# Moving the start addresses of pools by 32 or 64 bytes in a two-layer decoder kernel

## The chip, the cores and the metric

The kernel runs on one core of one Trainium2 chip. The metric is the device time of one execution in microseconds (us). The kernel before takes 2033.95 us, the median of three runs (2031.35 to 2036.37).

## What is computed

Two decoder layers on a sequence of 512 tokens with 1024 features, all in float32. Each layer is a half-step SwiGLU feed-forward network (FFN), a token mixer, and a second half-step FFN. The mixer of layer 0 is a short gated convolution, that of layer 1 a sparse attention with 16 heads in 4 groups.

```python
for i in range(DEPTH):                                # 2 layers
    h = adaln(x, norm_g[i, 0], shift[:, 0], scl[:, 0])
    x = x + HALF * gate[:, 0, None, :] * swiglu(h, ffn_w_in[i, 0], ffn_w_out[i, 0])
    h = adaln(x, norm_g[i, 1], shift[:, 1], scl[:, 1])
    y = short_conv_mixer(...) if i % 2 == 0 else nsa_mixer(...)
    x = x + gate[:, 1, None, :] * y
    h = adaln(x, norm_g[i, 2], shift[:, 2], scl[:, 2])
    x = x + HALF * gate[:, 2, None, :] * swiglu(h, ffn_w_in[i, 1], ffn_w_out[i, 1])
```

`swiglu` is `(silu(h @ w_g) * (h @ w_u)) @ w_out` with an inner width of 2816, which is 22 blocks of 128.

## The kernel before

**Data.** Everything is held transposed: a tile has 128 features on the partitions and 512 tokens along the free dimension, so that one partition of such a tile is 2048 bytes. Each float32 operand is split into a high and a low part (`split`, L163 to L165: ScalarE copies the high part, VectorE subtracts for the low part), and one product of two such operands is three matmuls, high by high, low by high and high by low (`mm3`, L167 to L170). In a name such as `gu<-hhi,whi` the profile gives the output, then the streamed operand (`hhi`), then the operand that is held in the array (`whi`). The streamed operand has 256 or 512 columns of 4 bytes, the held one has 128 columns, 512 bytes on a partition. `project` (L184) runs the three matmuls over the 8 blocks of 128 features.

**Stages in order.** FFN 0 (`ffn_first`), convolution (`conv`), FFN 1 and FFN 2 (`ffn`), attention (`nsa` with `compressor`, `attend`), FFN 3 (`ffn`). TensorE runs one instruction list in the order in which the scheduler put it.

**FFN 1, 2 and 3.** The first three of the 22 blocks are multiplied plainly (`head_start` and `pair`, matmuls of 256 columns, with `hs` and `gu` as outputs). The other 19 go through `seven_products` (L471): the two halves of the inner dimension and of the tokens make a 2 by 2 by 2 product that is done with seven products instead of eight, each of 4 by 3 = 12 matmuls of 256 columns. That makes 84 matmuls for each block j, 57 such blocks in the kernel, in this order: two products of `hhi`/`hlo` with `whi`/`wlo`, four of `th`/`tl` with `qah`/`qal` or `qbh`/`qbl`, and one of `hhi`/`hlo` with `qbh`/`qbl`. The blocks come in four parts (3, 6, 6 and 4 blocks). After each of the first three parts stand 144 matmuls of 512 columns, `y<-ahi/alo,whi/wlo`, which multiply the part's result by the output weights; after the last part the same work is done in matmuls of 256 columns (`ty`).

**FFN 0 and the convolution** use plain matmuls of 512 columns (`gu`, `y`, `cv`), with weights that come in turn from the common pool `wp` and from a pool of their own (`ap`).

**Pools.** Tiles lie in pools that are stacked from the left end of the memory (`cst`, `wp`, `tp`, `sp`, then `ada` or `hp`, `hw`, `sw`, `nw`, ...) and from its right end (`fa`, `tt`, `swa`, `tf`, `cva`, `na`, `ow`). A tile begins at the next multiple of 32 bytes, so the start of a tile within 128 bytes follows from the sizes of all that lie outside it. Those places are written here as two numbers, streamed/held: 96/64 says that the streamed tile begins 96 bytes and the held one 64 bytes behind a multiple of 128. Further columns or blocks of these tiles lie multiples of 512 bytes further on, so one pair of numbers holds for all matmuls of a product.

Of the kernel before, what the change touches and what calls it, by code (L numbers as in the profile page):

```python
# [12 lines left out]
F32 = mybir.dt.float32  # L13
F32R = mybir.dt.float32r
I32 = mybir.dt.int32
AF = mybir.ActivationFunctionType
# [5 lines left out]
P = 128  # L22
# [10 lines left out]
HD = 64  # L33
# [19 lines left out]
def decoder_kernel(ctx, tc, xT, cT, ng, adaw, adab, ffi, ffo, cwi, cw, cwo,  # L53
                   nwi, nwg, pos, w1, w2, qg, kg, nwo, rb, onehot, rowok, out):
    nc = tc.nc

    def pool(es, name, bufs, **kw):
        kw.setdefault("reuse_waits", "tile")
        return es.enter_context(tc.tile_pool(name=name, bufs=bufs, **kw))

    cst = pool(ctx, "cst", 1)
    wp = pool(ctx, "wp", 4)
    tp = pool(ctx, "tp", 1)
# [14 lines left out]
    def tmp(name, n=T, tag="t"):  # L78
        bufs, size = TAGS[tag]
        return tp.tile([P, n], F32, name=name, tag=tag, padded_shape=[P, size], bufs=bufs)  # L80
# [3 lines left out]
    ap = ada_es.enter_context(tc.tile_pool(name="ada", bufs=4))  # L84
# [6 lines left out]
    nc.sync.dma_start(cond, bass.AP(tensor=cT.tensor, offset=cT.offset, ap=[[0, P], [1, D]]))  # L91
    nc.gpsimd.dma_start(ngs, ng)
    nc.gpsimd.dma_start(adabs, adab)
    one = ap.tile([P, 1], F32, name="one", bufs=1)
    nc.vector.memset(one, 1.0)
    nc.scalar.activation(one, one, AF.Silu)
    ident = cst.tile([P, P], F32, name="ident")
    make_identity(nc, ident)
    ones = cst.tile([P, P], F32, name="ones")
# [1 line left out]
    cws = cst.tile([P, 3 * KD], F32, name="cws")  # L101
    qgs = cst.tile([P, 1], F32, name="qgs")
    kgs = cst.tile([P, 3], F32, name="kgs")
    rowm = cst.tile([P, 1], F32, name="rowm")
    mods = cst.tile([P, NSUB * NMOD], F32, name="mods")

    nc.scalar.activation(cond, cond, AF.Silu)
# [55 lines left out]
    def split(src, hi, lo):  # L163
        nc.scalar.activation(hi, src, AF.Copy)  # L164
        nc.vector.tensor_tensor(lo, src, hi, ALU.subtract)  # L165
# [6 lines left out]
    def weights(src, nk, ncol, own=None, held=3, raws=None, to=None):  # L172
        def part(name, dt, bufs, from_):
            return (from_ or wp).tile([P, nk * ncol], dt, name=name, tag=name, padded_shape=[P, KD * P], bufs=bufs)

        hi, lo = to or (part("whi", F32R, held, own), part("wlo", F32R, held, own))
        raws = raws or own
        raw = part("wraw", F32, 3 if raws in (None, wp) else 2, raws)
        nc.sync.dma_start(raw.rearrange("p (a n) -> p a n", a=src.shape[1]), src)
        split(raw, hi, lo)  # L180
        return [t.rearrange("p (k n) -> p k n", n=ncol) for t in (hi, lo)]
# [160 lines left out]
    def head_start(nrm, h, jobs):  # L342
        os = [psum("hs") for _ in jobs]
        for hf, (a, b) in enumerate(HALVES):
            with tc.high_priority():
                for d in range(KD):
                    nrm.piece(d, hf)
            for k in range(KD):
                for o, job in zip(os, jobs):
                    w, wc, kw = job(k)  # L350
                    project(o[:, a:b], w, wc, h, [(kw, k)], k == 0, k == KD - 1, a, b)
        return os
# [109 lines left out]
    def ffn(s, f, nrm, nxt, w0, ahead):  # L462
        with ExitStack() as es:
# [69 lines left out]
            with ExitStack() as tf_es:  # L533
                nrm.alloc_seven(hp, pool(tf_es, "tf", 1), tt)
                h = nrm.hi, nrm.lo
                with ExitStack() as hw_es:
                    hw = pool(hw_es, "hw", 1)
                    w = w0 + [weights(ffi[f, j, c], KD, P, hw, 1, wp) for j, c in js[len(w0):]]
                    os = head_start(nrm, h, [(lambda k, w=w_: (w, 0, k)) for w_ in w])
                os += pair(f, nj, h, halves=True)  # L540
                nrm.quarters()
            nj += 1
            sw_es = es.enter_context(ExitStack())
            sw = pool(sw_es, "sw", 1)
            for j in range(nj):
                hid.activate(os[2 * j], os[2 * j + 1])
            for p, (j0, j1) in enumerate(FOUR):
                for j in range(max(j0, nj), j1):
                    seven_products(j)
                n = j1 - j0  # L550
# [116 lines left out]
    def nsa_in(c, own=None, held=2):  # L667
        return [weights(nwi[c, kh], KD // 2, CW, own if kh else None, held if kh and own else 3, wp if held == 1 else None)
                for kh in range(2)]

    def nsa(s, nrm, nxt, w0, ahead):
        with ExitStack() as es:
# [46 lines left out]
            def squares():  # L719
                return sp.tile([P, 16], F32, name="vq")  # L720
# [57 lines left out]
            Q = [na.tile([P, T], F32R, name=f"q{q}") for q in range(NG)]  # L778
            keys, heads = turners(qn, kn, K, Q)
            with ExitStack() as hw_es:  # L780
                wv = nsa_in(5, pool(hw_es, "hw", 1), 1)
                os = head_start(nrm, h, [(lambda k, w=w, A=A: (w[k // 4], A, k % 4)) for w in (w0, wv) for A in range(2)])
            with ExitStack() as es2:
                nw = pool(es2, "nw", 1)
                compress = compressor(es2, os, kch, kcl, vcc)
                c0, c1 = compress(0), compress(1)
                vq, vk0, vk1 = squares(), squares(), squares()
                q0 = natural(0, raw(query_tiles(0), vq))
                next(c0)
                next(c0)  # L790
                next(c1)
                run(q0)
                normed(qn[0], vq)
                run(natural(8, raw(kn[0], vk0), nw))
                next(c0)
                normed(kn[0], vk0)
                next(c1)
                k1 = natural(6, raw(kn[1], vk1), nw)
                run(k1[:1])
                next(c0)  # L800
                run(k1[1:])
                normed(kn[1], vk1)
                next(c1)
                heads(0, 0)
                g = gates(es2, h, gsb)
                next(g)
                next(c0, None)
                heads(0, 1)
                v1 = natural(7, values(vn[1]), nw)
                run(v1[:1])  # L810
                keys(0, 0)
                next(c1, None)
                next(g, None)
                run(v1[1:])
                keys(0, 1)
# [3 lines left out]
    def compressor(es, os, kch, kcl, vcc):  # L819
            cm = pool(es, "cm", 1)  # L820
# [9 lines left out]
            def compress(kv):  # L830
# [46 lines left out]
                for c in range(2):  # L877
                    nc.tensor.matmul(po[:, 0:HD], hT[:, c, :], w2s[:, c, :], start=(c == 0), stop=(c == 1))
                if kv == 0:
                    ksq = cm.tile([P, HD], F32, name="ksq")  # L880
                    kss = cm.tile([P, 1], F32, name="kss")
                    nc.scalar.activation(ksq, po[:, 0:HD], AF.Square, accum_out=kss)
                    v = cm.tile([P, 1], F32, name="kv_")
                    nc.vector.tensor_scalar(v, kss, 1.0 / HD, EPS, op0=ALU.mult, op1=ALU.add)
                    r = rsqrt(v, 1)
                    kd = cm.tile([P, 2, HD], F32, name="kd")
                    for c in range(2):
                        nc.vector.tensor_scalar(kd[:, c, :], po[:, 0:HD], r, None, op0=ALU.mult)
                    yield
                    pk = psum("pk", "o")  # L890
                    nc.tensor.transpose(pk[:, 0:P], kd.rearrange("p a b -> p (a b)"), ident)
                    nc.scalar.activation(kch, pk[:, 0:P], AF.Copy, scale=kgs[:, 2:3])
                    nc.vector.scalar_tensor_tensor(kcl, pk[:, 0:P], kgs[:, 2:3], kch, op0=ALU.mult, op1=ALU.subtract)
                else:
                    split(po[:, 0:HD], vcc[:, 0, :], vcc[:, 1, :])
# [404 lines left out]
```

## Time and profile before

| | before |
|---|---|
| median of three runs | 2033.95 us (2031.35 to 2036.37) |
| the profiled execution | 2035.68 us, of which 2033.9 us are the span of its instructions |
| TensorE busy with matmuls | 1962.4 us, 96% of the span |
| VectorE, ScalarE, GpSimd busy | 1494.8, 875.3, 202.1 us |
| mean granted TensorE clock | 0.988 of full speed |

The span runs from the first to the last instruction. A matmul's row in the trace has a start and a duration. Matmuls overlap in the array's pipeline, so that the duration (0.28 us at 256 columns) is longer than the time from one start to the next (0.11 us); the time that a run of matmuls takes is the distance of their starts. That distance, for one matmul, is called its spacing below.

### The profile page before, as it was taken

Reading aid. Unit: us, or ns where it says so; the run is one execution under the profiler, and the core shown is the slowest. Engines: PE = TensorE matmul, PEld = TensorE weight load, DVE = VectorE, ACT = ScalarE, POOL = GpSimd, SP = SyncE. Lnnn points to the kernel's source line nnn. Section 1 sums busy time; section 2 is a strip of 40 time slices with the busy share of each in tenths; the row PEclk is TensorE's granted clock in tenths of the full one; section 3 lists DMA queues with packets and bytes.
Section 4 is the critical chain, followed back from the end, with each engine's and each line's share of the span. In section 5 each row is a group of like instructions: output and inputs, shape, how many; then the busy total and the mean of one; then the engine's idle time right before and its main releaser. Section 6 shows DMA issues by size and latency. Waiting matters only on the chain.

```text
span 2033.9 us, 32445 instructions
## 1 busy us (share of the span) xinstructions
PE 1962.4 (96%) x12644; PEld 1766.0 (87%) x12644; DVE 1494.8 (73%) x2597; ACT 875.3 (43%) x1410; POOL 202.1 (10%) x279
## 2 busy tenths in 40 slices
PE   5999999999998999999999999999999898999999
PEld 3878888888897898999989899999888788898989
DVE  7888888664467586768768676886887886686865
ACT  3322222332244343434534343455777755343532
POOL 0000000100011000000100000002354520000000
PEclk9999999999998999999999999999999999999999
DMA  8889988322237464533646453133111125565621
GB/s 303 301 311 320 333 317 323 141 97 83 83 84 199 123 171 137 153 114 84 184 137 172 137 153 113 45 137 104 53 51 49 58 63 142 145 169 146 167 78 63
DMA packets 113046, 307.39 MB, mean 151 GB/s; under 512 B 13883, under 2 KB 14155, under 8 KB 112892
## 3 DMA queue, kind: packets, MB, share of 16 engines
q1 hardware_dynamic: 97164, 274.81, 39.2%
q0 software_dynamic: 15728, 30.51, 8.6%
q8 instruction: 99, 1.62, 0.3%
q14 instruction: 55, 0.45, 0.1%
HBM read 302.12 MB, written 3.15 MB: 150 GB/s over the span
## 4 chain that ended last, share of the span: by engine, by line
PE 83%; DVE 8%; ACT 4%; DMA 2%; issue 2%; SPq 0%; POOL 0%; ACTq 0%; DVEq 0%; POOLq 0%
PE gu L168 13%; PE gu L169 13%; PE gu L170 13%; PE y L168 7%; PE y L169 7%; PE y L170 7%; PE cv L169 2%; PE cv L168 2%; PE hs L168 2%; PE hs L169 2%; PE cv L170 2%; PE hs L170 2%; DVE wlo L165 1%; PE ty L169 1%; PE ty L168 1%
## 5 line engine op out<-in xcount | busy, mean ns | idle before, releaser
L164 ACT ACTIVATE whi<-wraw 128x1024 fp32r<-128x1024 f32 (+2 forms) x286 | 285.3, 1001 | 552.0 <-PE y L169 262.8
L165 DVE TENSOR_TENSOR wlo<-wraw,whi 128x1024 fp32r<-128x1024 f32 (+2 forms) x286 | 330.0, 1157 | 65.2 <-ACT whi L164 62.1
L168 PE MATMUL gu<-hhi,whi 128*128 128x256 f32 (+1 forms) x856 | 273.8, 320 | 4.3 <-ACT whi L164 4.2
L169 PE MATMUL gu<-hlo,whi 128*128 128x256 f32 (+1 forms) x856 | 273.8, 320 | 0.0
L170 PE MATMUL gu<-hhi,wlo 128*128 128x256 f32 (+1 forms) x856 | 272.0, 318 | 0.2 <-DVE wlo L165 0.2
L168 PE MATMUL y<-ahi,whi 128*128 128x512 f32 x587 | 230.6, 395 | 0.2 <-ACT ahi L164 0.2
L170 PE MATMUL y<-ahi,wlo 128*128 128x512 f32 x587 | 230.7, 396 | 0.0
L169 PE MATMUL y<-alo,whi 128*128 128x512 f32 x587 | 230.4, 395 | 0.0
L119 DVE CUSTOM_DVE_ANT_0 adaraw<-adaraw,cond 128x1024 f32<-128x1024 f32 x144 | 173.4, 1222 | 21.1 <-DMA adaraw<-in_adaw 20.0
L168 PEld LDWEIGHTS gu<-hhi,whi 128*128 128x128 f32 x856 | 161.5, 189 | 19.8 <-ACT whi L164 5.6
L169 PEld LDWEIGHTS gu<-hlo,whi 128*128 128x128 f32 x856 | 161.4, 189 | 13.1
L170 PEld LDWEIGHTS gu<-hhi,wlo 128*128 128x128 f32 x856 | 160.8, 188 | 13.7 <-DVE wlo L165 0.6
L488 POOL DMA_DIRECT2D qa<-in_ffi x57 | 68.6, 1204 | 838.2 <-DVE qal L165 240.1
L168 PE MATMUL gu<-th,qah 128*128 128x256 f32 x456 | 130.1, 285 | 12.3 <-ACT p L515 12.3
L168 PEld LDWEIGHTS y<-ahi,whi 128*128 128x128 f32 x587 | 109.5, 188 | 29.2 <-ACT ahi L164 3.3
L169 PEld LDWEIGHTS y<-alo,whi 128*128 128x128 f32 x587 | 110.2, 188 | 27.9 <-DVE alo L165 1.8
L170 PEld LDWEIGHTS y<-ahi,wlo 128*128 128x128 f32 x587 | 110.2, 188 | 25.6
L557 DVE SCALAR_TENSOR_TENSOR x<-y,mods,x 128x512 f32<-128x512 f32 x72 | 54.0, 750 | 106.2 <-PE y L170 106.2
L168 PE MATMUL gu<-th,qbh 128*128 128x256 f32 x456 | 128.2, 281 | 2.4 <-ACT qbh L164 2.4
L169 PE MATMUL gu<-tl,qah 128*128 128x256 f32 x456 | 129.5, 284 | 0.0
L170 PE MATMUL gu<-th,qbl 128*128 128x256 f32 x456 | 128.4, 282 | 0.7 <-DVE qbl L165 0.7
L170 PE MATMUL gu<-th,qal 128*128 128x256 f32 x456 | 129.0, 283 | 0.0
(295 smaller groups left out, 5146.9 us busy)
## 6 DMA issues: line engine op xcount, KB each, us to landing
adaraw<-in_adaw SPq DMA_DIRECT2D x144, 512.0 KB, 5.6
wraw<-in_ffi SPq DMA_DIRECT2D x119, 512.0 KB, 3.7
qa<-in_ffi SPq DMA_DIRECT2D x114, 256.0 KB, 3.9
qa<-in_ffi POOLq DMA_DIRECT2D x57, 512.0 KB, 5.7
wraw<-in_ffo SPq DMA_DIRECT2D x72, 384.0 KB, 3.8
a<-in_ffi SPq DMA_DIRECT2D x57, 256.0 KB, 3.6
wraw<-in_cwi SPq DMA_DIRECT2D x24, 512.0 KB, 3.3
wraw<-in_nwi SPq DMA_DIRECT2D x20, 512.0 KB, 3.4
```

Source lines behind the costliest of these rows:

```text
L119: nc.vector.tensor_tensor_reduce(out=raw, in0=raw, in1=cond, scale=1.0, scalar=0.0, op0=ALU.mult, op1=ALU.add, accum_out=m)
L164: nc.scalar.activation(hi, src, AF.Copy)
L165: nc.vector.tensor_tensor(lo, src, hi, ALU.subtract)
L168: nc.tensor.matmul(o, sh, mh, start=first, stop=False)
L169: nc.tensor.matmul(o, sh, ml, start=False, stop=False)
L170: nc.tensor.matmul(o, sl, mh, start=False, stop=last)
L488: nc.gpsimd.dma_start(qa, bass.AP(tensor=a21.tensor, offset=a21.offset, ap=[a21.ap[0], [0, 2], a21.ap[1]]), accum_op=ALU.add)
L557: nc.vector.scalar_tensor_tensor(x[d], o, mod(s, 2, d), x[d], op0=ALU.mult, op1=ALU.add)
```

## The change

Only addresses change. On every engine the same instructions stand in the same order before and after; two small tiles move house.

- A pool `edge` of 32 bytes is opened first at the right end, so that every right-hand pool begins 32 bytes lower: what lay at 96 lies at 64.
- The pools `hw`, `sw` and `nw` get a first tile of 64 bytes that nothing uses: what lay at 64 in them lies at 0.
- The tile `one` (4 bytes, in the pool `ada`) goes, and `rowm` in `cst` is used in its place for the first SILU; `rowm` stands earlier in `cst`, and what follows it there shifts by 32 bytes. The weights in the pool `ada` move from 96 to 64.
- `ksq` is taken out of `cm` and becomes one of the four rotating tiles of `tp`.

| matmuls | columns | number | before | after |
|---|---|---|---|---|
| `y` of FFN 1 to 3 | 512 | 1296 | 96/0 | 64/0 |
| FFN 0 and conv, weights in `wp` | 512 | 1129 | 96/0 | 64/0 |
| FFN 0 and conv, weights in `ap` | 512 | some 990 | 96/96 | 64/64 |
| seven products: `hhi,whi` (24 for each j) | 256 | 1368 | 64/0 | 64/0 |
| seven products: `th,qa` and `th,qb` (48) | 256 | 2736 | 96/64 | 64/0 |
| seven products: `hhi,qb` (12) | 256 | 684 | 64/64 | 64/0 |
| `hs`, weights in `hw` | 256 | some 190 | 64/64 | 64/0 |
| `ty`, weights in `wp` | 256 | 281 | 96/0 | 64/0 |
| `ty`, weights in `tt` | 256 | some 280 | 96/96 | 64/64 |
| `ty` of conv, weights in `tw` | 256 | 141 | 96/32 | 64/0 |
| `ty` of conv, weights in `wp` | 256 | some 130 | 96/0 | 64/0 |
| `nat` (attention's inputs), weights in `wp` | 256 | 693 | 0/64 | 0/64 |
| `nat`, weights in `nw` | 256 | 140 | 64/64 | 0/64 |
| `gl` | 512 | 24 | 64/0 | 64/0 |

```diff
+    def shift(p, n):
+        p.tile([P, n // 4], F32, name="shift")
+
+    shift(pool(ctx, "edge", 1, side="right"), 32)
     cst = pool(ctx, "cst", 1)
...
-    one = ap.tile([P, 1], F32, name="one", bufs=1)
-    nc.vector.memset(one, 1.0)
-    nc.scalar.activation(one, one, AF.Silu)
+    rowm = cst.tile([P, 1], F32, name="rowm")
+    nc.vector.memset(rowm, 1.0)
+    nc.scalar.activation(rowm, rowm, AF.Silu)
...
-    rowm = cst.tile([P, 1], F32, name="rowm")
...
                     hw = pool(hw_es, "hw", 1)
+                    shift(hw, 64)
...
             sw = pool(sw_es, "sw", 1)
+            shift(sw, 64)
...
-                wv = nsa_in(5, pool(hw_es, "hw", 1), 1)
+                hw = pool(hw_es, "hw", 1)
+                shift(hw, 64)
+                wv = nsa_in(5, hw, 1)
...
                 nw = pool(es2, "nw", 1)
+                shift(nw, 64)
...
-                    ksq = cm.tile([P, HD], F32, name="ksq")
+                    ksq = tmp("ksq", HD)
```

## Rows read from the trace of the kernel before

**Rows 1.** The page: the span, TensorE's line of busy times, and the chain of work that ended last by engine.

```profile
span 2033.9 us, 32445 instructions
PE 1962.4 (96%) x12644; PEld 1766.0 (87%) x12644; DVE 1494.8 (73%) x2597; ACT 875.3 (43%) x1410; POOL 202.1 (10%) x279
...
PE 83%; DVE 8%; ACT 4%; DMA 2%; issue 2%; SPq 0%; POOL 0%; ACTq 0%; DVEq 0%; POOLq 0%
```

**Rows 2.** The waits of TensorE over the whole span, the longest three in total (who waited, for whom: us in total, times, longest us).

```profile
PE pr L270 <- DVE nacc L268: 14.4, 1, 14.4
PE gu L168 <- ACT p L515: 12.3, 3, 7.0
PE pr L278 <- DVE dg L277: 5.1, 1, 5.1
```

**Rows 3.** Busy time of the engines by stretch (stretch, its us, then PE, PEld, DVE, ACT, POOL busy with the number of instructions, granted clock, share of the DMA engines, GB/s): FFN 1, FFN 2, FFN 3 up to its last `ty`, and FFN 0.

```profile
614.00:952.00 338.00, 330.32 (x2337) 307.85 (x2338) 243.05 (x342) 139.19 (x191) 22.82 (x19) 0.98 0.52 148
952.00:1307.00 355.00, 351.24 (x2517) 328.53 (x2516) 263.33 (x388) 155.21 (x217) 24.04 (x19) 0.99 0.47 135
1674.00:2007.00 333.00, 325.22 (x2320) 303.18 (x2319) 240.98 (x331) 142.99 (x193) 20.40 (x17) 0.99 0.47 133
66.00:408.00 342.00, 341.62 (x1541) 278.64 (x1539) 277.13 (x437) 99.47 (x127) 6.31 (x4) 1.00 0.81 291
```

**Rows 4.** The longest wait of ScalarE between 66 and 364 us (FFN 0).

```profile
ACT whi L164 <- PE gu L169: 113.8, 30, 4.5
```

**Rows 5.** The timeline of TensorE (start us, duration us, instruction) over one block j of the seven products in FFN 1: the first matmul of each of the seven products and the first of the next block. Between two rows stand 11 matmuls.

```profile
802.38 0.28 PE L168 MATMUL gu<-hhi,whi 128*128 128x256 f32 x1
...
803.74 0.28 PE L168 MATMUL gu<-hhi,whi 128*128 128x256 f32 x1
...
805.10 0.29 PE L168 MATMUL gu<-th,qah 128*128 128x256 f32 x1
...
806.51 0.28 PE L168 MATMUL gu<-th,qah 128*128 128x256 f32 x1
...
807.91 0.28 PE L168 MATMUL gu<-th,qbh 128*128 128x256 f32 x1
...
809.31 0.28 PE L168 MATMUL gu<-th,qbh 128*128 128x256 f32 x1
...
810.71 0.29 PE L168 MATMUL gu<-hhi,qbh 128*128 128x256 f32 x1
...
812.15 0.28 PE L168 MATMUL gu<-hhi,whi 128*128 128x256 f32 x1
```

**Rows 6.** The same timeline at two places where 64/0 matmuls of 256 columns follow on something else: the plain blocks of FFN 1, 94 matmuls behind a wait in which the clock had fallen (first and last start), and the first two products of the first block j behind a `y` (three starts, 12 matmuls apart).

```profile
619.25 0.28 PE L168 MATMUL gu<-hhi,whi 128*128 128x256 f32 x1
...
630.32 0.28 PE L168 MATMUL gu<-th,qah 128*128 128x256 f32 x1
...
792.48 0.28 PE L168 MATMUL gu<-hhi,whi 128*128 128x256 f32 x1
...
793.89 0.28 PE L168 MATMUL gu<-hhi,whi 128*128 128x256 f32 x1
...
795.30 0.28 PE L168 MATMUL gu<-th,qah 128*128 128x256 f32 x1
```

**Rows 7.** The timeline of TensorE at 96/0 with 512 columns: 18 matmuls of `y` in FFN 1 (first start and the next after them), and 24 of `gu` in FFN 0 (the same).

```profile
771.48 0.39 PE L168 MATMUL y<-ahi,whi 128*128 128x512 f32 x1
...
775.68 0.39 PE L168 MATMUL y<-ahi,whi 128*128 128x512 f32 x1
...
170.21 0.39 PE L168 MATMUL gu<-hhi,whi 128*128 128x512 f32 x1
...
175.81 0.40 PE L168 MATMUL gu<-hhi,whi 128*128 128x512 f32 x1
```

**Rows 8.** The timeline of TensorE at 64/0 with 512 columns, the only place where they stand in a row: `gl` in the attention's inputs, 18 matmuls from the first of these starts to the second.

```profile
1377.90 0.39 PE L170 MATMUL gl<-hhi,wlo 128*128 128x512 f32 x1
...
1382.02 0.39 PE L170 MATMUL gl<-hhi,wlo 128*128 128x512 f32 x1
```

**Rows 9.** The timeline of TensorE at 96/96 with 512 columns, `gu` in FFN 0: the second, the tenth and the last start of a run of 24 (8 and 14 matmuls apart).

```profile
176.04 0.40 PE L169 MATMUL gu<-hlo,whi 128*128 128x512 f32 x1
...
177.89 0.39 PE L168 MATMUL gu<-hhi,whi 128*128 128x512 f32 x1
...
181.06 0.40 PE L170 MATMUL gu<-hhi,wlo 128*128 128x512 f32 x1
```

**Rows 10.** The matmuls that stream the tile `pch` in the attention, 64/64 with 512 columns (number: shortest, median and longest duration in ns, first and last start in us), and from the page those of `y` (number, busy us, mean ns).

```profile
L1086 PE MATMUL o<-pch,vz x16: 391/396/397, 1437.4 to 1648.8; 128*128 128x512 f32 x16
...
L168 PE MATMUL y<-ahi,whi 128*128 128x512 f32 x587 | 230.6, 395 | 0.2 <-ACT ahi L164 0.2
```

**Rows 11.** The timeline of TensorE in `nat`, two runs of 24 matmuls each by their first start and the next after them: the first with 12 at 0/64 and 12 at 64/64, the second with all 24 at 0/64.

```profile
1342.83 0.29 PE L168 MATMUL nat<-whi,hhi 128*128 128x256 f32 x1
...
1345.63 0.29 PE L168 MATMUL nat<-whi,hhi 128*128 128x256 f32 x1
...
1404.25 0.28 PE L168 MATMUL nat<-whi,hhi 128*128 128x256 f32 x1
...
1406.97 0.28 PE L168 MATMUL nat<-whi,hhi 128*128 128x256 f32 x1
```

**Rows 12.** The page: the DMA issue of the seven products that GpSimd makes once for each block j (number, KB, us to landing).

```profile
qa<-in_ffi POOLq DMA_DIRECT2D x57, 512.0 KB, 5.7
```

## The prediction

> **What bounds the kernel now.** I read the page first: TensorE is busy for 1962.4 us of a span of 2033.9 us, and 83% of the chain that ended last is TensorE's own work [rows 1]. Then its waits: the longest three together are 31.8 us, and two of them stand at the start, where nothing is to be multiplied yet [rows 2]. The windows by stage show that no other engine is close in the FFNs: in FFN 1 VectorE is busy for 243 of 338 us, ScalarE for 139 [rows 3]. In FFN 0 VectorE (277 of 342 us) and the DMA engines (0.81) are fuller, but there ScalarE's longest wait, 113.8 us in 30 times, is for TensorE to free a weight tile [rows 4]; the others are ahead. So the kernel's time is the number of matmuls times their spacing, and a change of the spacing goes into the time nearly whole.
>
> The timeline then shows that the spacing is not one number. In one block j of the seven products all 84 matmuls have the same shape, nothing waits, and yet the first two products take 1.36 us each, the next four 1.40 to 1.41, the last 1.44 [rows 5]: 113.3, 117 and 120 ns for one matmul. They differ in where their tiles begin: 64/0, 96/64 and 64/64. At 512 columns 96/0 takes 4.20 us for 18, and 5.60 us for 24, 233.3 ns each [rows 7]; 64/0 takes 4.12 us for 18, 228.9 ns [rows 8]; 96/96 takes 5.02 us for 22, 228.2 ns, and 226.4 over the last 14 of them [rows 9]. So the place of a tile within 128 bytes is worth up to 6%.
>
> But the place is not all. The same 64/0 matmuls at 256 columns stand at two spacings: 113.3 ns in [rows 5], and 11.07 us for 94, 117.8 ns, in the plain blocks behind a wait; behind a `y` it is 1.41 us for a product of 12, 117.5 ns [rows 6]. Each spacing holds as long as the run lasts, so it is set by what went before. In [rows 5] that is the 64/64 product that ends the block before (1.44 us here too). I call them the quick and the slow pace of 64/0.
>
> **The change part by part.** No instruction is added, and none is moved. The memset and the SILU that used `one` use `rowm`, in the first microseconds. `ksq` takes one of four rotating tiles where TensorE has other work. Both I cost at nothing; their cover is the wait of 14.4 us at the start for the first, and for the second the attention's inputs, where each is a fraction of a microsecond. That the targets of DMAs and the operands of VectorE and ScalarE shift by 32 bytes too I also cost at nothing: they would have to be slower by the slack above to be seen. What remains is five terms of spacing.
>
> *Seven products.* 57 blocks [rows 12], of which 12 are the first of a part. A block takes 9.77 us, the first of a part 9.90 us (the products of [rows 5], and 2 x 1.41 + 4 x 1.41 + 1.44 with [rows 6]; the four in the middle at the slow pace too are my estimate). Together 45 x 9.77 + 12 x 9.90 = 558.5 us. After the change all 84 are 64/0. At the slow pace a block takes 84 x 117.8 ns = 9.89 us, 57 of them 563.9 us: **+5.4 us**. At the quick pace it is 84 x 113.3 = 9.52 us, 542.5 us: -16 us. I take the slow one: it is what 64/0 does after a wait and after a `y` [rows 6], these are the two ways into the seven products, and the 64/64 product, behind which the quick pace stands, is gone. In the first two products of a block the change then loses what the four in the middle hold or win.
>
> *`y` of FFN 1 to 3.* 1296 matmuls go from 233.3 to 228.9 ns [rows 7, 8]: **-5.7 us**. The bounds are 226.4 ns, the best spacing that any 512 columns have [rows 9], -8.9 us, and no change. I take `gl`, since it is the same pair of places.
>
> *FFN 0 and convolution, weights in `wp`.* 1129 matmuls with the same move: **-5.0 us**, with bounds -7.8 and 0. That is worth its price only if the DMA engines follow; their share of 0.81 [rows 3] would go to 0.83.
>
> *The same, weights in their own pool.* 990 matmuls go from 96/96 to 64/64. At 256 columns the two pairs should be alike, since in both the tiles begin at one place. At 512 the only 64/64 is `pch`, with a median duration of 396 ns [rows 10]; durations run 162 ns above the spacing (395 ns for `y` at 233.3), so that would be 234 ns. `pch` stands alone among matmuls of other sizes, so I take the neighbour's 228.2 [rows 9]: **0**, with bounds +5.7 us (990 x 5.8 ns) and -1.8 us (226.4 ns).
>
> *Small ones.* `nat`: 12 runs of 24 go from 2.80 to 2.72 us [rows 11], -1.0 us. `ty`: 281 matmuls at 96/0 and 270 of the convolution, from some 120 ns (an estimate: 64/64 in [rows 5]) to 117.8, -1.2 us; and 190 in `hs` the same, -0.4 us. Together **-2.6 us**; at the quick pace of 113.3 they would be another -3.3 us. Attention itself: 0, with bounds of 3 us both ways, an estimate: some 500 of its matmuls change their pair, by up to the 6 ns between 113.3 and 120.
>
> The sum is +5.4 - 5.7 - 5.0 + 0 - 2.6 = -7.9 us. The profiled execution took 2035.7 us, 1.8 us above its span, and would take 2027.8; it lies 1.7 us above the median of the runs shown, 2033.95, so the median to expect is 2026.
>
> Here the Trainium skill speaks against the change. What the rows show is above: one shape, three spacings. In "SBUF — State Buffer", in the section on the DMA port swizzle, it says that the memory has lines of 16 bytes and that consecutive accesses within a line have full bandwidth, so that what counts is the stride. By that a contiguous stream that begins at a multiple of 32 bytes is as good at 96 as at 64, and the change would give 0 us. "TensorE: Matmul & The Clock Gate" (section "Wait — 56ns, not 53.3ns?") gives a warm spacing of 215.7 ns at 512 columns, with no word on addresses. [Rows 7, 8, 9] have 233.3, 228.9 and 226.4 to 228.2 at a granted clock of 1.00 [rows 3], so the trace does not agree with it.
>
> **The rivals.**
>
> *Quick pace throughout.* If the seven products come out at 113.3 ns, the sum is -16 - 8.9 - 7.8 - 2.6 - 3.3 = -38.6 us, 1995. For it: the quick pace, once there, lasts for whole products [rows 5]; one event in a part would be enough, and the `y` that stands before a part is no longer 96/0, but 64/0, from which no row shows the entry. Against it: a wait led to the slow pace [rows 6], and waits stay, at the first blocks above all [rows 2].
>
> *Half and half.* Some parts quick, others slow, as 64/0 is in the trace of before. With half the blocks quick the seven products give (5.4 - 16) / 2 = -5.3 us, and the sum is -5.3 - 5.7 - 5.0 - 2.6 - 1.6 = -20.2 us, 2014.
>
> *Slower.* The 64/64 product goes, and with it the only thing that brings 64/0 to the quick pace. The slow pace holds in the seven products (+5.4 us), 512 columns have a slow pace of 64/0 too, at the 233.3 ns of 96/0 (0 instead of -10.7 us), and 64/64 at 512 columns is at `pch`'s 234 ns (+5.7 us): with the small ones +8.5 us, 2042. It decides, once 64/64 has `pch`'s price, where the 2425 matmuls of 512 columns at 64/0 come out above 229.8 ns (8.5 us / 2425 = 3.5 ns below 233.3). For it speaks `pch`; against it `gl`, which stood at 228.9 ns behind a wait.
>
> *Nothing.* The spacings of [rows 5] come from something else that goes by product, for example from which tiles lie far apart, and not from the place within 128 bytes: 0 us, 2034. This is what the 16-byte rule would give too. Against it: `nat` and `hhi,whi` have quite different tiles and are at 113.3 ns both, in the two mirrored pairs 0/64 and 64/0 [rows 5, 11].
>
> **How the numbers follow.** Slow pace (forecast, 2026, between 2018 and 2034 by the bounds of its terms): 0.42. Quick throughout: 0.25. Half and half: 0.15. Slower: 0.10. Nothing: 0.08. About 0.3% (6 us) can be told from no change, so faster is below 2027.8. The forecast lies near that: I give 0.6 of it to faster and 0.4 to the same. Faster is 0.25 + 0.15 + 0.25 = 0.65; the same 0.17 + 0.08 = 0.25; slower 0.10. The range goes from 1991, which takes in most of the quick case with its bounds, to 2036: outside remain the slower case and the far end of the quick one, some 2 in 10.
>
> **What would show it.** In the timeline of after: the seven products at 9.89 us for a block and 117.8 ns for every matmul, the first two products at 1.41 us where they had 1.36. A block of 9.52 us is the quick case, and its first occurrence tells what brings it. `y` at 4.12 us for 18; `gu` of FFN 0 with its own weights at 5.5 us for 24 (5.6 is `pch`'s price); `nat` at 2.72 us throughout. If TensorE's waits grow by more than 3 us, the cover was thinner than the windows say, and FFN 0 is the place to look.

## The result and the profile after

The changed kernel takes 2010.36 us, the median of 4 runs (2003.76, 2008.76, 2011.96, 2016.58), against 2033.83 us before (median of 4, 2031.35 to 2036.37): a ratio of 0.9884, 95% interval 0.9849 to 0.9919. The profiled execution is the fastest of the four, so its rows describe a run 6.6 us below the median. One execution of the kernel edge_only below took 6045.61 us, three times as long as its other nine, and the ratio there leaves it out. The lines of the helpers stand 4 further down than before (`mm3` is L172 to L174).

The page of after, as in [rows 1]: the span, the busy times, the chain that ended last; and the longest waits of TensorE, as in [rows 2].

```profile
span 2002.0 us, 32444 instructions
PE 1929.8 (96%) x12644; PEld 1745.2 (87%) x12644; DVE 1493.5 (75%) x2597; ACT 873.9 (44%) x1410; POOL 203.2 (10%) x279
...
PE 78%; DVE 9%; DMA 5%; ACT 4%; issue 2%; SPq 1%; POOL 0%; DVEq 0%; ACTq 0%; POOLq 0%
```

```profile
PE pr L274 <- DVE nacc L272: 13.5, 1, 13.5
PE gu L172 <- ACT p L519: 10.8, 2, 5.6
```

The same number of matmuls keeps TensorE busy for 32.6 us less, and the span is shorter by 31.9 us. What TensorE does not fill of the span is 72.2 us, where it was 71.5, though the chain that ended last goes less often through it (78% for 83%). Not all of the 31.9 us is spacing at one clock: the mean granted clock is 0.992 in this execution and 0.988 in that of before, which is 33 us at the lower of its two levels here and 50 us there.

The timeline of TensorE over one block j in FFN 1 (start us, duration us, instruction; 11 matmuls lie between two rows), as in [rows 5].

```profile
803.44 0.28 PE L172 MATMUL gu<-hhi,whi 128*128 128x256 f32 x1
...
804.80 0.28 PE L172 MATMUL gu<-hhi,whi 128*128 128x256 f32 x1
...
806.16 0.28 PE L172 MATMUL gu<-th,qah 128*128 128x256 f32 x1
...
807.52 0.28 PE L172 MATMUL gu<-th,qah 128*128 128x256 f32 x1
...
808.88 0.28 PE L172 MATMUL gu<-th,qbh 128*128 128x256 f32 x1
...
810.24 0.28 PE L172 MATMUL gu<-th,qbh 128*128 128x256 f32 x1
...
811.60 0.28 PE L172 MATMUL gu<-hhi,qbh 128*128 128x256 f32 x1
...
812.96 0.28 PE L172 MATMUL gu<-hhi,whi 128*128 128x256 f32 x1
```

All seven products take 1.36 us: 113.3 ns, the quick pace, and 9.52 us for the block where [rows 5] have 9.77. There is no 64/64 product any more, and the pace is quick all the same. The first block behind a `y` and the beginning of the second, as in the second half of [rows 6]:

```profile
693.41 0.28 PE L172 MATMUL gu<-hhi,whi 128*128 128x256 f32 x1
...
703.31 0.28 PE L172 MATMUL gu<-hhi,whi 128*128 128x256 f32 x1
...
706.13 0.28 PE L172 MATMUL gu<-th,qah 128*128 128x256 f32 x1
...
707.49 0.28 PE L172 MATMUL gu<-th,qah 128*128 128x256 f32 x1
```

The first block takes 9.90 us, 117.8 ns a matmul, the slow pace that was forecast. So do two products of the second block (2.82 us together). Then, at the first matmul of the third product, the pace turns (1.36 us), and it stays quick for the 396 matmuls to the end of the part. Over three traces of this kernel there are 27 such parts behind a `y`, counted from all starts: 20 turn within a matmul of the third product of the second block, 5 within some four matmuls of that of the first, 2 are quick from their first matmul, and none falls back. So of the 25 that begin slow, 5 turn in the first block and all the others at the same place of the second.

512 columns: 18 matmuls of `y` in FFN 1 and 24 of `gu` in FFN 0 with weights in `wp`, 64/0 ([rows 7] before), and 24 of `gu` with weights in their own pool, 64/64 ([rows 9] before).

```profile
771.92 0.39 PE L172 MATMUL y<-ahi,whi 128*128 128x512 f32 x1
...
776.04 0.39 PE L172 MATMUL y<-ahi,whi 128*128 128x512 f32 x1
...
168.48 0.39 PE L172 MATMUL gu<-hhi,whi 128*128 128x512 f32 x1
...
173.97 0.39 PE L172 MATMUL gu<-hhi,whi 128*128 128x512 f32 x1
...
179.41 0.39 PE L172 MATMUL gu<-hhi,whi 128*128 128x512 f32 x1
```

These are 4.12 us (228.9 ns, as in [rows 8]), 5.49 us (228.8) and 5.44 us (226.7).

### The profile page after: what moved, and what is told of

Same layout as the page of the kernel before. It is cut to its first block, busy times and chain, and to the rows that moved or that the text cites. A ratio compares the mean times of both kernels' runs of the same rounds, so it can differ in the third digit from the quotient of the medians.

```text
span 2002.0 us, 32444 instructions
## 1 busy us (share of the span) xinstructions
PE 1929.8 (96%) x12644; PEld 1745.2 (87%) x12644; DVE 1493.5 (75%) x2597; ACT 873.9 (44%) x1410; POOL 203.2 (10%) x279
## 4 chain that ended last, share of the span: by engine, by line
PE 78%; DVE 9%; DMA 5%; ACT 4%; issue 2%; SPq 1%; POOL 0%; DVEq 0%; ACTq 0%; POOLq 0%
PE gu L172 11%; PE gu L174 11%; PE gu L173 11%; PE y L172 7%; PE y L173 7%; PE y L174 7%; DMA adaraw<-in_adaw 2%; DVE wlo L169 2%; PE cv L172 2%; PE cv L173 2%; PE cv L174 2%; PE hs L172 2%; PE hs L173 2%; PE hs L174 2%; DMA qa<-in_ffi 2%
## 5 line engine op out<-in xcount | busy, mean ns | idle before, releaser
L172 PE MATMUL gu<-hhi,whi 128*128 128x256 f32 (+1 forms) x856 | 273.3, 319 | 5.9 <-ACT whi L168 5.9
L174 PE MATMUL gu<-hhi,wlo 128*128 128x256 f32 (+1 forms) x856 | 271.6, 318 | 0.7 <-DVE wlo L169 0.7
L172 PE MATMUL y<-ahi,whi 128*128 128x512 f32 x587 | 230.0, 394 | 0.3 <-ACT ahi L168 0.3
L174 PE MATMUL y<-ahi,wlo 128*128 128x512 f32 x587 | 227.8, 391 | 0.0
L123 DVE CUSTOM_DVE_ANT_0 adaraw<-adaraw,cond 128x1024 f32<-128x1024 f32 x144 | 174.1, 1222 | 25.6 <-DMA adaraw<-in_adaw 24.1
L172 PEld LDWEIGHTS gu<-hhi,whi 128*128 128x128 f32 x856 | 161.4, 188 | 20.1 <-ACT whi L168 7.1
L174 PEld LDWEIGHTS gu<-hhi,wlo 128*128 128x128 f32 x856 | 161.0, 188 | 13.4 <-DVE wlo L169 1.1
L172 PE MATMUL gu<-th,qah 128*128 128x256 f32 x456 | 128.5, 282 | 10.8 <-ACT p L519 10.8
L172 PEld LDWEIGHTS y<-ahi,whi 128*128 128x128 f32 x587 | 109.5, 188 | 27.8 <-ACT ahi L168 4.5
L174 PEld LDWEIGHTS y<-ahi,wlo 128*128 128x128 f32 x587 | 110.2, 188 | 24.3
L172 PE MATMUL gu<-th,qbh 128*128 128x256 f32 x456 | 127.2, 279 | 3.1 <-ACT qbh L168 3.1
L174 PE MATMUL gu<-th,qal 128*128 128x256 f32 x456 | 128.0, 281 | 0.0
L174 PE MATMUL gu<-th,qbl 128*128 128x256 f32 x456 | 127.2, 279 | 0.5 <-DVE qbl L169 0.5
```

What stands on the lines that cost most here:

```text
L123: nc.vector.tensor_tensor_reduce(out=raw, in0=raw, in1=cond, scale=1.0, scalar=0.0, op0=ALU.mult, op1=ALU.add, accum_out=m)
L172: nc.tensor.matmul(o, sh, mh, start=first, stop=False)
L174: nc.tensor.matmul(o, sl, mh, start=False, stop=last)
```

## The experiments

Each was timed beside the kernel before on the same chip; ratios below are against that. The theory grew in two steps. After the first four runs the place within 128 bytes no longer accounted for the spacings, and from then on the runs are read by the **distance**: the start of the streamed tile less the start of the held one, modulo 256 bytes. Read from the addresses of the compiled kernels:

| kernel | distance in `y` | `hhi,whi` | `th,q` | `hhi,qb` | mean spacing in ns, same order |
|---|---|---|---|---|---|
| before | 96 | 64 | 32 | 0 | 233.6; 114.2; 117.1; 119.4 |
| after | 64 | 64 | 192 | 192 | 229.1; 114.8; 114.0; 113.9 |
| edge_only | 64 | 64 | 0 | 0 | 229.3; 115.7; 120.0; 119.9 |
| no_edge | 96 | 64 | 224 | 192 | 233.6; 115.1; 118.2; 116.5 |
| mirror | 192 | 64 | 64 | 192 | 233.4; 114.9; 117.8; 114.6 |
| reset | 64 | 64 | 192 (qa), 128 (qb) | 128 | 229.2; 117.7; 118.1; 118.8 |
| edge160 | 192 | 64 | 64 | 192 | 233.4; 114.6; 117.7; 114.5 |
| sw192 | 64 | 64 | 64 | 64 | 229.2; 117.3; 117.3; 117.3 |
| a128 | 0 | 64 | 192 | 192 | 227.5; 114.5; 113.5; 113.5 |

The means are worked out from the starts of all matmuls of a trace, where no wait stands between two of them.

**edge_only: the edge pool alone, in the kernel before.**

```diff
+    shift(pool(ctx, "edge", 1, side="right"), 32)
```

> Only the right-hand pools move (by 32 bytes). Theory (the pair of places within 128 bytes sets the spacing): y of FFN 1 to 3 goes from 96/0 to 64/0, 233 to 229 ns; in the seven products th,qa and th,qb go from 96/64 to 64/64, so that a block is 2 x 1.36 + 5 x 1.44 = 9.92 us instead of 9.77. Sum: +7 (seven products), -5.7 (y), -1.8 (y of FFN 0), some -0.6 (ty): about -1 us against the kernel before, 2033. Rival (the gain goes with the right-hand pools as such, or comes from waits): between the kernel after and the kernel before, 2010 to 2025, with th,qa below 117 ns.

Measured: 2039.64 us, ratio 1.0019 (1.0008 to 1.0031). One block of FFN 1 on the timeline of edge_only:

```profile
804.96 0.28 PE L172 MATMUL gu<-hhi,whi 128*128 128x256 f32 x1
...
807.67 0.28 PE L172 MATMUL gu<-th,qah 128*128 128x256 f32 x1
...
813.43 0.28 PE L172 MATMUL gu<-hhi,qbh 128*128 128x256 f32 x1
...
814.88 0.28 PE L172 MATMUL gu<-hhi,whi 128*128 128x256 f32 x1
```

Four products take 5.76 us and the last 1.45, 120 ns a matmul, and the two at the start of the block, behind such a product, 2.71 us, 113 ns. `y` gains its 4.4 ns, and the products at 64/64 take it back. That holds for the parts behind a `y` in FFN 1. From the second part of FFN 2 on most blocks take 10.03 us, for the first two products are slow behind the same 64/64 product:

```profile
1079.25 0.28 PE L172 MATMUL gu<-hhi,whi 128*128 128x256 f32 x1
...
1082.08 0.28 PE L172 MATMUL gu<-th,qah 128*128 128x256 f32 x1
```

These 24 take 2.83 us, 117.9 ns. Of the blocks that follow on a 64/64 product without a wait 21 begin slow and 21 quick, so a 64/64 product does not by itself bring the quick pace.

**no_edge: the change without the edge pool.**

```diff
-    shift(pool(ctx, "edge", 1, side="right"), 32)
```

> The kernel after without the 32 bytes at the right end: the left-hand pools move alone. Theory: the seven products have 96/0 in their four middle products, 119.8 ns as ty has it, so a block is 4 x 1.44 + 3 x 1.36 to 1.41 = 9.84 to 9.98 us, +4 to +12 us in 57 blocks; y stays at 233 ns; the gu and cv of FFN 0 and conv gain 768 x 4.5 ns = -3.5 us. Sum 0 to +8: 2034 to 2042. Rival (the left-hand shifts alone bring the gain): 2015 or less.

Measured: 2032.48 us, ratio 0.9985 (0.9971 to 0.9998). The four `th` products of a block of FFN 2, on the timeline of no_edge:

```profile
1096.46 0.28 PE L171 MATMUL gu<-th,qah 128*128 128x256 f32 x1
...
1102.13 0.28 PE L171 MATMUL gu<-hhi,qbh 128*128 128x256 f32 x1
```

`y` stays at 233.6 ns, and the `th` products take 5.67 us, 118.1 ns, and not the 119.8 expected, so the time lies below the 2034 to 2042 that I expected. Neither part is worth much alone, +4.8 and -2.3 us, where both together give -23.5: the gain is in the pair of places, not in the sum of two shifts.

**mirror: both operands exchanged, 0/64 wherever the change has 64/0.**

```diff
+    shift(pool(ctx, "edge", 1, side="right"), 96)
     cst = pool(ctx, "cst", 1)
+    shift(cst, 64)
...
+    ap.tile([P, 16], F32, name="apart", bufs=1)
...
             hp = pool(es, "hp", 1)
+            shift(hp, 64)
```

(and the rest as in the change)

> All pairs turned round: 0/64 where the kernel after has 64/0, 64/0 in nat, and 0/64 for the weights in the own pool of FFN 0 and conv. Theory (0/64 has only the quick pace, since nat came to 113.3 ns each time, also behind a wait): the seven products at 9.52 us for every block, also the first of a part, -7 us against the kernel after; 512 columns at 226.6 to 229 ns, 0 to -6 us. Time 1997 to 2003, and single runs closer together than the 13 us of the kernel after, if their spread comes from when the pace turns. Rival (the two directions are alike): as the kernel after, 2010, with slow stretches at the beginning of each part.

Measured: 2036.01 us, ratio 1.0008 (0.9992 to 1.0023). A block of FFN 1, and 18 matmuls of `y`, on the timeline of mirror:

```profile
817.73 0.28 PE L174 MATMUL gu<-hhi,whi 128*128 128x256 f32 x1
...
820.45 0.28 PE L174 MATMUL gu<-th,qah 128*128 128x256 f32 x1
...
826.10 0.28 PE L174 MATMUL gu<-hhi,qbh 128*128 128x256 f32 x1
...
827.47 0.28 PE L174 MATMUL gu<-hhi,whi 128*128 128x256 f32 x1
```

```profile
772.79 0.40 PE L174 MATMUL y<-ahi,whi 128*128 128x512 f32 x1
...
776.99 0.40 PE L174 MATMUL y<-ahi,whi 128*128 128x512 f32 x1
```

`y` takes 4.20 us for 18, as at 96/0, and the four `th` products take 5.65 us, slow in every block, in most blocks between products that are quick: the same pair of places 0/64 at two spacings in one block. The theory's 1997 to 2003 us is missed by 33 us. With that the place within 128 bytes was in doubt as the cause; edge160 and own0 below refute it at 512 columns.

**reset: the change with a 64/64 product put back (`qbh`, `qbl` 64 bytes further).**

```diff
                 ah_, al_ = (sw.tile([P, 2, QT], F32R, name=f"qa{e}", bufs=2) for e in "hl")
+                sw.tile([P, 16], F32, name="apart")
```

> The kernel after with qb 64 bytes further on: the last three products of a block (th,qb twice, hhi,qb) are 64/64, the first four 64/0. Theory (a 64/64 product at 120 ns brings the 64/0 behind it to the quick pace): from the second block of a part on the first four products at 1.36 us in every block, the last three at 1.44: 9.76 us a block. Against the kernel after, whose 64/0 averages 114.6 ns (9.62 us), +8 us: 2018. Rival (the quick pace comes from something else than the 64/64 product): slow first products in several blocks, 9.9 us a block, 2025.

Measured: 2032.28 us, ratio 0.9988 (0.9968 to 1.0007). Two block starts and the first `th,qb` between them, on the timeline of reset:

```profile
1795.99 0.28 PE L172 MATMUL gu<-hhi,whi 128*128 128x256 f32 x1
...
1801.65 0.28 PE L172 MATMUL gu<-th,qbh 128*128 128x256 f32 x1
...
1805.92 0.28 PE L172 MATMUL gu<-hhi,whi 128*128 128x256 f32 x1
```

Four products of 64/0 take 5.66 us, 117.9 ns, and three of 64/64 take 4.27 us, 118.6. A 64/64 product stands before each block and the block is slow: my reason for the quick pace of [rows 5] is refuted here too. The third product, too, turned the pace at only 4 of 53 slow entries here (11 of 19 in the first trace of after).

**edge160: the change with 160 bytes at the edge in place of 32.** All places within 128 bytes remain.

```diff
-    shift(pool(ctx, "edge", 1, side="right"), 32)
+    shift(pool(ctx, "edge", 1, side="right"), 160)
```

> The changed kernel with the edge pool at 160 bytes in place of 32: every pair keeps its place within 128 bytes (64/0), but th and ahi begin at 320 in place of 448 within 512 bytes; hhi stays at 448, the held tiles at 128 (whi) and 0 (qah, qbh). In the changed kernel the pace turned from 117.8 to 113.3 ns only at the entry into the third product, where the distance from held to streamed tile (modulo 256 bytes) goes from 64 to 192. Theory: what gives the pace its chance to turn is a change of that distance. Here it stays at 64 from hhi,whi to th,qah and th,qbh, and becomes 192 only at hhi,qbh, the seventh product: the turns stand there and nowhere at the third; the first blocks lose 4 products more than in the changed kernel, 9 parts x 48 x 4.5 ns = 2 us, so about 2012 us. Rival: the turn hangs on the held tile's own move from 128 to 0, or on the third product as such: turns at the third product, 2010 us. Second rival: only places within 128 bytes matter and the turn is chance: turns anywhere in a block, 2004 to 2017 us. In all cases 512 columns at 229 ns.

Measured: 2028.59 us, ratio 0.9954 (0.9937 to 0.9971), 14.6 us slower than the changed kernel beside it. A block of FFN 1, and 18 matmuls of `y`, on the timeline of edge160:

```profile
809.03 0.28 PE L172 MATMUL gu<-hhi,whi 128*128 128x256 f32 x1
...
811.75 0.28 PE L172 MATMUL gu<-th,qah 128*128 128x256 f32 x1
...
817.40 0.28 PE L172 MATMUL gu<-hhi,qbh 128*128 128x256 f32 x1
...
818.77 0.28 PE L172 MATMUL gu<-hhi,whi 128*128 128x256 f32 x1
```

```profile
772.49 0.40 PE L172 MATMUL y<-ahi,whi 128*128 128x512 f32 x1
...
776.69 0.40 PE L172 MATMUL y<-ahi,whi 128*128 128x512 f32 x1
```

The turn stands at the seventh product, where the distance goes from 64 to 192, and nowhere at the third: the theory's place. (Three of the nine parts behind a `y` are quick from their first matmul.) Two things I had not foreseen cost the rest. `y` is at 64/0 and takes 233.3 ns, so its gain goes by the distance too (192 here, 64 in the change). And at `th` the pace falls back to 117.7 ns, with the distance 64 unchanged; there the streamed tile's own place changes. The block is that of mirror to 0.01 us (9.74), with the same four distances and the places within 128 exchanged.

**sw192: the change with `sw` 192 bytes further in place of 64.** Places within 128 remain; the distance is 64 in all seven products.

```diff
-            shift(sw, 64)
+            shift(sw, 192)
```

> The changed kernel with the pool sw 192 bytes in place of 64 further: 64/0 within 128 bytes everywhere as in the changed kernel, but qah, qal, qbh, qbl begin at 128 within 512 bytes, where whi and wlo begin too. So neither the held tile's place nor its distance to the streamed tile (64 modulo 256) changes within a block. Theory (the turn needs a change of the distance): no turn in any block, all 84 matmuls stay at 117.8 ns, 9.89 us for a block, against a mean of some 114.6 ns in the changed kernel: 57 x 84 x 3.2 ns = +15 us, 2025 us; 512 columns at 229 ns as there. Rival (the turn is chance, or comes from what other engines do at that time, since ScalarE splits a tile there): turns in the first or second block as in the changed kernel, 2004 to 2017 us.

Measured: 2025.92 us, ratio 0.9936 (0.9921 to 0.9951), as the theory had it. The first block behind a `y` in FFN 1 and the start of the next, on the timeline of sw192:

```profile
784.13 0.28 PE L172 MATMUL gu<-hhi,whi 128*128 128x256 f32 x1
...
794.03 0.28 PE L172 MATMUL gu<-hhi,whi 128*128 128x256 f32 x1
```

A block of 9.90 us, all slow. Of the nine parts behind a `y` eight are slow from the first matmul to the last (504 of them in the longest), and one is quick from the first to the last (504). Nothing turns within these parts, where neither the distance nor the place of either tile changes and no wait stands between.

**own0: the change with the weights of FFN 0's and the convolution's own pool at 64/0 in place of 64/64**, by 64 bytes in `ap` and 64 in two `hp`.

```diff
+    ap.tile([P, 16], F32, name="apart", bufs=1)
...
             hp = pool(es, "hp", 1)
+            shift(hp, 64)
```

> The changed kernel with the weights of FFN 0 and of the convolution in their own pool at 64/0 in place of 64/64: some 990 matmuls of 512 columns and 170 of 256. In the trace of the changed kernel 64/64 at 512 columns has a mean of 227.4 ns and 64/0 has 228.9. By that: 990 x 1.5 ns = +1.5 us, 2012 us. Rival (the price of pch was the right one and 64/64 is slower where it stands among its own kind): -5 us, 2005 us.

Measured: 2016.98 us, ratio 0.9892 (0.9876 to 0.9908), 3 us above the changed kernel beside it, with intervals that overlap. Runs of 24 `gu` in FFN 0 on the timeline of own0, the first with weights in `wp`, the second with its own:

```profile
170.13 0.39 PE L173 MATMUL gu<-hhi,whi 128*128 128x512 f32 x1
...
175.72 0.40 PE L173 MATMUL gu<-hhi,whi 128*128 128x512 f32 x1
...
181.23 0.39 PE L173 MATMUL gu<-hhi,whi 128*128 128x512 f32 x1
```

5.59 us and 5.51 us. The first was meant to stay as it was, 5.49 us: by moving `hp`, its distance went from 64 to 192 (233 ns), again with the same places within 128.

**after_again and after_third: the changed kernel twice more.**

> The changed kernel once more, for a second trace. Its four times spread from 2003.8 to 2016.6 us, more than the kernel before does with 31 (2028.9 to 2041.5, but most within 2 us of the median). Theory: the spread comes from where the pace turns; a part that stays slow throughout costs 391 x 4.5 ns = 1.8 us, and one whose turn comes in the second block in place of the first 0.4 us. Then parts of an execution that is longer by t us hold t / 4.5 ns more slow matmuls. Rival: the turns stand at the same places, and the difference of some 6 us lies in the attention, which took 233 us in some traces and 239 us in others.

> The changed kernel a third time, on the same chip as the version with ahi at 128, for the comparison of the two. The first two medians were 2010.4 and 2014.0 us. Theory (most turns of the pace stand at the entry into the third product, of the first or second block of a part, and the rest of the spread lies in the attention): again one of these in every part, mean spacing of all 64/0 at 256 columns 114.6 ns, 2010 to 2015 us. Rival (the first trace was a lucky one): parts that stay slow, a mean above 115.5 ns.

Measured: 2014.03 us, ratio 0.9874 (0.9853 to 0.9894), and 2010.63 us, ratio 0.9889 (0.9871 to 0.9906). The mean spacing of 64/0 at 256 columns is 114.6, 114.6 and 114.5 ns in the three traces, so the spread does not come from the turns. The first theory of it falls; of after_third's the part on the turns holds (but for one part that is quick from the start), the part on the attention does not: it takes 233.2, 231.8 and 235.5 us, whereas FFN 0 takes 338.2, 343.1 and 344.5 us and FFN 3 without its last `ty` 325.7, 329.6 and 329.2. Those hold 10 of the 12.6 us by which after_third's profiled execution is longer than the first. An instance of FFN 0 on the timeline of after_third:

```profile
369.08 0.79 PE L172 MATMUL y<-ahi,whi 128*128 128x512 f32 x1 [3.58 <-ACT ahi L168]
...
371.04 0.63 PE L172 MATMUL y<-ahi,whi 128*128 128x512 f32 x1
371.47 0.63 PE L173 MATMUL y<-alo,whi 128*128 128x512 f32 x1
```

and the windows before it and in it (columns as in [rows 3]):

```profile
340.00:364.00 24.00, 24.00 (x107) 19.75 (x107) 19.28 (x31) 6.11 (x9) 0.00 (x0) 1.00 0.83 306
369.00:372.00 3.00, 2.77 (x6) 1.88 (x7) 2.93 (x7) 1.08 (x2) 0.00 (x0) 0.51 0.46 148
```

TensorE waits 3.58 us for `ahi`, and then starts matmuls 430 ns apart at a granted clock of 0.51, the lower of its two levels (1.2 GHz), where it had 1.00 before the wait. The mean granted clock of the three profiled executions is 0.992, 0.991 and 0.988, in the order of their times (2003.76, 2011.65, 2016.32 us). The longer executions of the other kernels mostly have the lower mean clock too (reset: 2027.43 us at 0.992, 2043.01 us at 0.985), so that much of the spread goes with time at the lower level. What makes the waits differ is open.

**a128: the change with `ahi` at 128 within 256 bytes, `th` where it was.** Distance 0 in `y`.

```diff
-    shift(pool(ctx, "edge", 1, side="right"), 32)
+    shift(pool(ctx, "edge", 1, side="right"), 96)
...
+            shift(pool(es, "gap", 1, side="right"), 192)
             tt = pool(es, "tt", 1, side="right")
```

> The changed kernel with the edge pool at 96 in place of 32 bytes and a gap of 192 bytes before tt: ahi and alo begin at 128 in place of 192 within 256 bytes, th and tl stay at 192. y (512 columns) then has its streamed and held tiles at 128 and 128 within 256, distance 0 in place of 64, and the places 0/0 within 128. Theory (512 columns go by the distance from held to streamed tile within 256 bytes: 227.0 ns at 0, 229.1 at 64, 232.3 at 128, 233.4 at 192 in the traces so far): y at 227.0 ns, 1697 x 2.1 ns = -3.6 us, 222 matmuls of y with their own weights at distance 192, +1.4 us; ty 288 x 3.3 ns = +1.0 us where its distance goes to 0 and -1 us where it leaves 0: in sum -2 us. The step from y into the seven products is now a change of the distance, so that the pace can turn there: at best all first blocks are quick, another -2.5 us; 2008 to 2012 us where the changed kernel has 2013. Rival (the place within 128 bytes of each tile, whatever the distance): the only 0/0 of 512 columns stood at 233 to 236 ns in all traces (34 and 35 matmuls of the attention); y then goes to 233 ns, 1697 x 4 = +7 us, 2020 us.

Measured: 2008.87 us, ratio 0.9864 (0.9843 to 0.9885). 18 matmuls of `y` and the first block behind it in FFN 1, on the timeline of a128:

```profile
774.51 0.39 PE L172 MATMUL y<-ahi,whi 128*128 128x512 f32 x1
...
778.59 0.39 PE L172 MATMUL y<-ahi,whi 128*128 128x512 f32 x1
...
782.67 0.28 PE L172 MATMUL gu<-hhi,whi 128*128 128x256 f32 x1
...
785.49 0.28 PE L172 MATMUL gu<-th,qah 128*128 128x256 f32 x1
...
792.29 0.28 PE L172 MATMUL gu<-hhi,whi 128*128 128x256 f32 x1
```

`y` takes 4.08 us, 226.7 ns, at 0/0, where the rival had 233. Two products are slow and then the pace turns, in all nine parts in the first block. The version has the lowest median here, but with 2010.63 for the change on the same chip, and intervals that overlap, it is not shown to be faster than that.

**The account.** The sum of all differences in spacing to the trace of before, and the medians against the kernel before on the same chip:

| kernel | spacings, us | median, us |
|---|---|---|
| after (three traces) | -27.9, -27.4, -28.2 | -23.5, -24.1, -25.6 |
| edge_only | +3.1 | +4.8 |
| no_edge | -4.4 | -2.3 |
| mirror | -3.0 | +1.2 |
| reset | -8.9 | -2.5 |
| edge160 | -9.3 | -9.6 |
| sw192 | -13.0 | -12.2 |
| own0 | -22.1 | -21.2 |
| a128 | -30.7 | -27.3 |

By which matmuls beside waits are left out, the sums move by about 1 us. From kernel to kernel the spacings give the order of the medians, and the size within some 6 us. The rest was not added up; it has to lie in waits and in time at the lower clock, of which reset, the furthest off, had more in its profiled execution (0.984) than before (0.988).

## Why the prediction was right, and where it was not

**What bounds the kernel** was right: a gain of 28 us in spacing appears as 23.5 to 25.6 us in the median. The sign was right. The range of 1991 to 2036 held the time because it took in the rivals; the forecast's own, 2018 to 2034, did not, and its upper end is not the sum of the bounds either (the three terms at 512 columns would carry it to 2042). The step to 2026 failed at its largest term.

**Seven products: forecast +5.4 us, measured -11.4.** From the means in the table 57 blocks take 558.3 us before (forecast 558.5) and 546.9 after. The failed step is "I take the slow one", with both of its reasons: that the 64/64 product brings the quick pace, and that the slow pace lasts through the part without it. The slow start came as forecast; then the pace turned at the third product. That the change of distance at that place gives the chance to turn to the quick pace is shown by sw192, which takes the change away (no turn in nine parts; the held tile stays in its place there too), and by edge160, where the held tile moves at the third product, and the streamed one with it, without a change of distance (no turn) and the turn stands where the distance does change. With the pace left slow the blocks take 561.6 us (sw192), where the forecast had 563.9: it priced a case that the change does not reach, since it shifts `sw` by 64 and not by 192. That sw192 takes 2025.9 us and the forecast was 2026 is luck: the one is 12.2 us below the kernel before on its chip, the other was to be 7.9 below.

**`y`, FFN 0 and convolution: forecast -5.7 and -5.0, together -10.7; measured -10.9** (1668 `y`, 456 `gu`, 239 `cv` and 51 `hs` go from 233.6 to 229.1 ns or nearly so). Mechanism and size were right, by [rows 8]; the bound of 226.4 ns was not reached. But the reason was too short. [Rows 8] and the changed `y` share not only 64/0 but the distance 64; at 64/0 with distance 192 (edge160) the term would have been 0.

**Own pool: forecast 0, measured -2.0 us**, a little beyond the lower bound of -1.8: 226.7 ns in a row. Both places, 96/96 and 64/64, are at distance 0, so these 2 ns are not accounted for by the distance. `pch` of [rows 10] did not carry over to matmuls among their own kind.

**Small ones: forecast -2.6, measured -3.9 us.** `ty` -1.5 (forecast -1.2; all of it in FFN 1 to 3, at the quick pace) and `hs` out of 64/64 and 96/0 -1.2 (-0.4) are there; `nat` gains nothing, +0.2 (-1.0), since its 0/64 came out slower, 114.4 to 115.2 ns; and some 550 `hs` that keep their place gain 1.4 us that were not forecast, since they are at the quick pace more often.

**Nothing for addresses of DMAs and of the other engines, and for the two tiles that moved,** was right as far as the waits tell: the first one went from 14.4 [rows 2] to 13.5 us. In FFN 0, the place that the prediction named, TensorE's waits went from nothing to 0.4, 2.2 and 3.8 us in the three traces, the last over the 3 us that were to be the sign of too thin a cover.

**The rivals.** *Half and half* (2014) came nearest, though not as I put it: the parts are not slow or quick, nearly all begin slow and turn; that its number fits so well is in part luck. *Quick throughout* (-38.6 us) had the right pace for most of each part. Of the 10.7 us by which the spacings miss it 10.4 are two terms: 512 columns at 229 and not 226.4 ns (16.7 - 10.9 = 5.8 us), and the slow starts of the parts (16 - 11.4 = 4.6 us). *Slower* failed at 512 columns, which are at 229.1 without a slow run. *Nothing* was right in its premise, that the place within 128 bytes is not what the spacing goes by, and wrong in its 0 us. Beside it stood the 16-byte rule in the Trainium skill's "SBUF — State Buffer" (section on the DMA port swizzle): by that rule a shift of contiguous tiles would give 0 us, and the runs show 23.5, so it does not describe what a matmul's reads cost here.

**What stays open.** Why a change of distance turns the pace at one entry and not at the next (11 of 19, 4 of 53), why the second block of a part turned where the first had not, in all 20 cases, why in edge160 and mirror the pace falls at `th` while the distance stays 64 (both tiles move there), and what in the memory makes 256 bytes the period. The distance as the cause at 512 columns is shown by edge160, mirror, own0 and a128, and neither tile's own place does as well: held at 128 modulo 256, the streamed tile at 128, 192 and 64 gives 227.5, 229.1 and 233.4 ns; streamed at 192, the held one at 192, 128 and 0 gives 226.7, 229.1 and 233.1. The paces at 256 columns are only located, not explained. Whether FFN 0 and FFN 3 wait more because of the change was not settled: the kernels above that are near the kernel before have 339.7 to 346.5 us in FFN 0 too.

## What to carry to other kernels

Where TensorE is the bound, read the spacing of matmuls from start to start, and set it beside where the two tiles begin: modulo 256 bytes, as a difference, not each for itself modulo 128. Two shifts that do little alone can do much together, so such a change is to be tried and costed as a pair. A row of a pace that has memory (the same matmuls at 113.3 and 117.8 ns) is no price for another place in the program until it is known what sets the pace; cost both and let the range hold them.

## What the hardware showed

At 512 columns, over all traces, the mean spacing goes by the distance of the two tiles modulo 256 bytes: 226.8 ns at 0 (192/192; 228.7 for 224/224; 227.5 in a128's `y` in the FFNs, with 128/128), 229.1 at 64 (192/128; 230.6 for both 64/0 and 128/64), 232.5 at 128, 233.0 to 233.4 at 192 (64/128, 128/192, 192/0), and 233.1 to 233.9 at 32, 96 and 224. (Here the pairs are streamed/held modulo 256.) Read modulo 512, distances of 0 and 256 have 226.8 and 227.4 ns, 192 and 448 have 233.4 and 233.1, 64 and 320 have 230.6 and 229.1: a period of 256 holds within 1.5 ns. Small groups of the attention, a few matmuls among other sizes, lie above that (232 to 236 ns at distance 0).

At 256 columns distance 0 has 120 ns in the seven products of edge_only, behind either pace (117.9 to 120.0 in smaller groups), and 64 and 192 have two paces each, 113.3 and 117.8 ns. At 64 either holds for hundreds of matmuls (504 at each in one trace of sw192). I had not expected a pace with such a memory, nor that it turns at the entry into a product, within one to four matmuls.
